# GpSimd's queue, in place of SP's, for the DRAM writes of the turned gates in a two-layer encoder trunk

## Chip, core and metric

The kernel runs on one NeuronCore of a Trainium2 chip. Its engines are TensorE (PE, with its weight loads shown apart as PEld), VectorE (DVE), ScalarE (ACT), GpSimd (POOL) and SyncE (SP); each takes its instructions in order and waits at semaphores. A DMA is issued by an instruction on some engine's queue, and instructions behind that one on the same engine follow it. The metric is the device time of one execution in microseconds, lower is better.

## What is computed

The reference runs a hidden state `h` of 256 tokens by 1024 channels through two layers, each a sandwich of feed-forward, mixer, feed-forward; the mixer is a convolution module in layer 0 and latent attention in layer 1. The change concerns the four feed-forwards:

```python
def swiglu_ffn(h, w1, w3, w2):
    return (jax.nn.silu(h @ w1) * (h @ w3)) @ w2
...
h = h + FFN_RES_WEIGHT * swiglu_ffn(rmsnorm(h, ffn_norm1[i]), ffn1_w1[i], ffn1_w3[i], ffn1_w2[i])
m = rmsnorm(h, mix_norm[i])
h = h + (conv_module(m, ...) if i % 2 == 0 else mla(m, positions, ...))
h = h + FFN_RES_WEIGHT * swiglu_ffn(rmsnorm(h, ffn_norm2[i]), ffn2_w1[i], ffn2_w3[i], ffn2_w2[i])
```

`w1` and `w3` are 1024 x 2816, `w2` is 2816 x 1024, all float32, and each is read from DRAM once.

## The kernel before

**Weights.** All weights stand in one list of blocks of 128 x 2048 float32 (1 MB) in the order of use. `load` (line 161) brings a block from DRAM into one of three `raw` buffers with a DMA on SP's queue (line 179), then splits it in two halves of 128 x 1024: ACT casts `hi` (line 187) and DVE takes the rest, `lo = raw - hi` (line 188), into one of five pairs of buffers. Each product is three TensorE instructions (`mm3`, lines 271 to 277): hi by low, hi by high, lo by high.

**A feed-forward** (`ffn_in`, line 637) has two stages. In the first, six chunks of gate columns are computed: `u = h @ w1` and `h @ w3` for two blocks of 128 tokens (tb 0 and 1), 512 columns in each of chunks 0 to 4 (four PSUM banks each), and 256 columns of both in chunk 5 (two banks). When a chunk's products are done, ACT takes silu from PSUM (`s`, line 721), DVE multiplies by the second half from PSUM (line 722), and `turn` (line 639) brings the gate into the layout with gate columns on the partitions. In the second stage `Rows` (line 570) multiplies the turned gates `Gh`, `Gl` by `w2` into four PSUM banks `o`, one for each token block and half of the output columns. The products `u`, `o` share the four banks of tag "A": the banks of `o(tb 1, d)` are those that chunk 5's two `u` tiles have just left.

**Turning a gate.** `turn_blocks` (line 344) turns a gate of 128 tokens by 512 columns in three steps. DVE transposes its 32 x 32 blocks (line 349) into `gt` (two buffers). Four DMAs (lines 352 and 353), one for each 32 partitions and of 64 KB, or 32 KB in chunk 5, write these blocks to a DRAM tile `gd` in rearranged order, as 32 x 4 pieces of 512 bytes. One DMA (line 357) reads the DRAM tile back as `gb`; it waits until the four writes have landed. Back in `turn`, ACT casts `Gh` from `gb` (line 646) and DVE subtracts for `Gl` (line 647). There are 12 gates in a feed-forward, thus 48 writes and 12 reads, and four feed-forwards: 192 writes and 48 reads. The same function, with the tag "h", turns part of `h` in front of three later stages (lines 404 to 411).

**The order.** A scheduler lays out each engine's instructions ahead of time, with some orders given by hand (`order`, `urgent`). So SP's queue is a fixed list of weight loads, gate writes and gate reads, and it stands still at the first one whose wait isn't met. DVE and ACT have fixed lists too, in which `Gh` and `Gl` stand between the casts of weights and the gates of the following chunk. GpSimd has little to do in the feed-forwards: a few 128 x 1 steps of norms, and in the first feed-forward 32 products `dpair` (line 1402) for the convolution.

Of the kernel before, what the change touches and what calls it, by code (L numbers as in the profile page):

```python
# [84 lines left out]
def trunk(ctx: ExitStack, tc: tile.TileContext, x, xt, first, pos, invf, gfin, wdw,  # L85
          f1w13, f1w2, f2w13, f2w2, cw1, cw2, wa, wuq, wukv, wo, wpair, out):
    nc = tc.nc
# [12 lines left out]
    def uid(s):  # L100
        n_uid[0] += 1
        return f"{s}_{n_uid[0]}"
# [34 lines left out]
    def order(ins, first):  # L137
        tc.add_manual_dep(ins.ins, first.name, mybir.DependencyInfo(
            mybir.DependencyClass.NoSync, mybir.DependencyReason.DATA), reason="order")
# [102 lines left out]
    for k in range(KT):  # L242
        c = slice(k % 4 * 512, k % 4 * 512 + 512)
# [100 lines left out]
    def turn_blocks(pool, src, n, tag, after=()):  # L344


        w = n * P
        t = pool.tile([P, 512], F32, tag=tag + "t", name=uid(tag + "t"), bufs=2)
        nc.vector.transpose(t[:, :w], src.rearrange("p (t j q) -> p j t q", t=n, q=32))  # L349
        d = dram.tile([P, w], F32, tag=tag + "d", name=uid(tag + "d"), bufs=4)  # L350
        dv = d.rearrange("(j p) (i c) -> i p j c", p=32, c=32 * n)
        for i in range(4):
            dma = nc.sync.dma_start(dv[i], t[32 * i:32 * i + 32, :w].rearrange("p (j c) -> p j c", j=4))
            for a in after:
                order(dma, a.ins)
        b = pool.tile([P, 512], F32, tag=tag + "b", name=uid(tag + "b"), bufs=2)
        last_read[0] = nc.sync.dma_start(b[:, :w], d)
        return b[:, :w].rearrange("p (i t q) -> p t i q", i=4, q=32)

    class Norm:  # L360
# [42 lines left out]
        @urgent  # L403
        def begin(self):

            raw_to(len(loaded) + RAW_BUFS)
            first = [dma for raw, dma in raws.values()]
            for q in range(2):
                self.turning.append(turn_blocks(self.pool, h[1][:, 512 * q:512 * q + 512], 4, "h", first))
                first = [last_read[0]]  # L410
                turns.extend(first)
# [225 lines left out]
    def ffn_in(act, X, make_next, beside):  # L637
        Gh = act.tile([P, NF, S], F32R, tag="Gh", name=uid("Gh"))
        Gl = act.tile([P, NF, S], F32R, tag="Gl", name=uid("Gl"))
        def turn(c, tb, w, g):  # L640

            n = w // P
            f = slice(4 * c, 4 * c + n)
            bv = turn_blocks(act, g[:, :w], n, "g")
            gh = Gh[:, f, tbs(tb)].rearrange("p t (i q) -> p t i q", q=32)
            nc.scalar.copy(gh, bv)  # L646
            nc.vector.tensor_sub(Gl[:, f, tbs(tb)].rearrange("p t (i q) -> p t i q", q=32), bv, gh.bitcast(F32))  # L647
# [874 lines left out]
```

## Time and profile before

| | |
|---|---|
| time, median of 3 runs | 918.64 us (918.57 to 919.02) |
| the profiled execution's own time | 918.66 us |
| its span, first to last instruction | 916.9 us |
| TensorE, weight loads, VectorE, ScalarE, GpSimd busy | 99%, 83%, 64%, 54%, 14% |
| DRAM traffic | 179.78 MB read, 14.16 MB written, 212 GB/s over the span |
| DMA queues | q1 "hardware_dynamic" moves 193.28 of 194.73 MB |

The profile shows one execution. A row of a timeline gives start, duration, engine, line, operation, the tile written and the tiles read, and how many such instructions were merged; the bracket behind it is the engine's idle time before it, with what ended it. "SPq" is a DMA issued on SP's queue, and its duration is that of the issue alone: the landing stands in a list of issues by line. A group's row gives the count, the total busy time, the mean of one in ns, and the idle time before. The "chain" of the profile goes back from the last instruction to what released each one.

### The profile page before, as it was taken

How to read it: one execution, taken by the hardware profiler on the slowest of the kernel's cores; microseconds unless marked ns; L12 is line 12 of the kernel's file. 1: busy time of each engine (PE TensorE's matmuls, PEld its weight loads, DVE VectorE, ACT ScalarE, POOL GpSimd, SP SyncE). 2: the span in 40 equal slices, each digit the busy share in tenths (PEclk: the TensorE clock that was granted, in tenths of full speed). 3: DMA queues.
4: the chain of work that ended last, by engine and by line, in shares of the span. 5: the costliest groups of instructions: out<-in, count | busy, mean ns of one | idle time of the engine just before them, and what ended most of it. 6: DMA issues, size and time to landing. Idle time of an engine off the chain costs nothing.

```text
span 916.9 us, 12087 instructions
## 1 busy us (share of the span) xinstructions
PE 908.8 (99%) x4337; PEld 764.4 (83%) x4337; DVE 590.8 (64%) x932; ACT 494.2 (54%) x845; POOL 126.8 (14%) x259
## 2 busy tenths in 40 slices
PE   9999999999999999999999999999999999999997
PEld 7888888898988888888888888888899888888886
DVE  6886764489987666655476666544768676566633
ACT  7564544388877444543364544434677574454432
POOL 1730000079951000000010000000400000000000
PEclk9999999999999999999999999999999999999999
DMA  9988776533227767776567777753445477776711
GB/s 332 315 271 284 265 265 218 193 138 139 93 77 269 251 230 236 251 232 221 184 212 267 246 247 241 234 209 135 156 155 184 147 253 277 249 250 219 255 48 46
DMA packets 65292, 194.73 MB, mean 212 GB/s; under 512 B 11728, under 2 KB 37200, under 8 KB 45904
## 3 DMA queue, kind: packets, MB, share of 16 engines
q1 hardware_dynamic: 64800, 193.28, 60.6%
q10 hardware_dynamic: 432, 0.69, 0.2%
q8 instruction: 34, 0.56, 0.2%
q14 instruction: 26, 0.21, 0.1%
HBM read 179.78 MB, written 14.16 MB: 212 GB/s over the span
## 4 chain that ended last, share of the span: by engine, by line
PE 97%; DMA 1%; ACT 0%; SPq 0%; DVE 0%; issue 0%; ACTq 0%
PE u L277 17%; PE u L273 17%; PE u L276 17%; PE o L277 10%; PE o L276 10%; PE o L273 10%; PE u L760 3%; PE gate L760 3%; PE o L995 2%; PE tp L317 1%; PE pairs L803 1%; DMA raw<-in_f1w 1%; PE a L276 1%; PE a L273 1%; PE a L277 1%; PE nope L277 1%
## 5 line engine op out<-in xcount | busy, mean ns | idle before, releaser
L188 DVE TENSOR_TENSOR lo<-raw,hi 128x1024 fp32r<-128x1024 f32 (+1 forms) x292 | 344.4, 1219 | 172.5 <-ACT hi L187 171.7
L187 ACT CAST hi<-raw 128x1024 fp32r<-128x1024 f32 x294 | 292.6, 1047 | 240.6 <-PE o L277 82.0
L273 PE MATMUL u<-lo,Xh 128*128 128x512 f32 x688 | 268.0, 389 | 0.2 <-DVE lo L188 0.2
L276 PE MATMUL u<-hi,Xh 128*128 128x512 f32 x688 | 267.7, 389 | 0.0
L277 PE MATMUL u<-hi,Xl 128*128 128x512 f32 x688 | 267.6, 389 | 0.0
L273 PEld LDWEIGHTS u<-lo,Xh 128*128 128x128 f32 x688 | 129.1, 188 | 27.3 <-DVE lo L188 0.6
L277 PEld LDWEIGHTS u<-hi,Xl 128*128 128x128 f32 x688 | 129.1, 188 | 27.2 <-DVE Xl L336 0.5
L276 PEld LDWEIGHTS u<-hi,Xh 128*128 128x128 f32 x688 | 129.1, 188 | 26.8
L276 PE MATMUL o<-hi,Gh 128*128 128x512 f32 (+1 forms) x356 | 137.9, 387 | 0.0
L277 PE MATMUL o<-hi,Gl 128*128 128x512 f32 (+1 forms) x356 | 137.8, 387 | 0.0
L273 PE MATMUL o<-lo,Gh 128*128 128x512 f32 (+1 forms) x356 | 137.2, 387 | 0.0
L308 POOL TENSOR_TENSOR ms<-ss 128x1 f32<-128x1 f32 x16 | 9.2, 576 | 586.6 <-ACT junk L300 586.6
L276 PEld LDWEIGHTS o<-hi,Gh 128*128 128x128 f32 x356 | 66.9, 188 | 13.6
L273 PEld LDWEIGHTS o<-lo,Gh 128*128 128x128 f32 x356 | 66.9, 188 | 13.5
L277 PEld LDWEIGHTS o<-hi,Gl 128*128 128x128 f32 x356 | 66.9, 188 | 13.4
L647 DVE TENSOR_TENSOR Gl<-gb,Gh 128x512 fp32r<-128x512 f32 (+1 forms) x48 | 31.3, 652 | 61.0 <-ACT Gh L646 61.0
L646 ACT CAST Gh<-gb 128x512 fp32r<-128x512 f32 (+1 forms) x48 | 28.0, 583 | 78.4 <-DMA gb<-gd 78.4
L849 DVE SCALAR_TENSOR_TENSOR acc<-V,dw,acc 128x128 f32<-128x128 f32 (+1 forms) x174 | 53.9, 390 | 0.0
L870 ACT ACTIVATE prod<-V,dw 128x128 f32<-128x128 f32 (+1 forms) x128 | 45.6, 416 | 1.8 <-POOL Y L871 1.0
L722 DVE TENSOR_TENSOR s<-s,u 128x512 f32<-128x512 f32 (+1 forms) x48 | 30.5, 634 | 7.6 <-PE u L277 7.6
L721 ACT ACTIVATE s<-u,R 128x512 f32<-128x512 f32 (+1 forms) x48 | 31.2, 649 | 5.0 <-PE u L277 3.7
L349 DVE STREAM_TRANSPOSE gt<-s 128x512 f32<-128x512 f32 (+1 forms) x48 | 32.0, 666 | 1.4
(222 smaller groups left out, 858.6 us busy)
## 6 DMA issues: line engine op xcount, KB each, us to landing
raw<-in_f2w SPq DMA_DIRECT2D x66, 1024.0 KB, 5.0
raw<-in_f1w SPq DMA_DIRECT2D x62, 1024.0 KB, 5.3
raw<-in_cw SPq DMA_DIRECT2D x12, 1024.0 KB, 4.8
gd<-gt SPq DMA_DIRECT2D x160, 64.0 KB, 3.5
gb<-gd SPq DMA_DIRECT2D x40, 256.0 KB, 4.6
raw<-in_wo SPq DMA_DIRECT2D x4, 1024.0 KB, 4.9
raw<-in_wuq SPq DMA_DIRECT2D x3, 1024.0 KB, 4.7
raw<-in_f1w SPq DMA_DIRECT2D x8, 256.0 KB, 4.7
```

The source lines that it names most:

```text
L187: casts[len(loaded), i] = (nc.scalar.copy(hi[:, c], raw[:, c]), low.tensor_sub(lo[:, c], raw[:, c], hi[:, c].bitcast(F32)))
L188: low.tensor_sub(lo[:, c], raw[:, c], hi[:, c].bitcast(F32)))
L273: mm = nc.tensor.matmul(o, ah, bl, start=start, stop=False)
L276: nc.tensor.matmul(o, ah, bh, start=False, stop=False)
L277: return nc.tensor.matmul(o, al, bh, start=False, stop=stop)
L349: nc.vector.transpose(t[:, :w], src.rearrange("p (t j q) -> p j t q", t=n, q=32))
L647: nc.vector.tensor_sub(Gl[:, f, tbs(tb)].rearrange("p t (i q) -> p t i q", q=32), bv, gh.bitcast(F32))
L721: nc.scalar.activation(s[:, :w], u[0, tb][:, :w], AF.Silu, scale=X.r[tb])
L722: nc.vector.tensor_mul(s[:, :w], s[:, :w], u[0, tb][:, w:] if both else u[1, tb])
L760: mm = nc.tensor.matmul(u[:, t], w[:, c], X.x[:, k, t], start=(k == 0), stop=(k == KT - 1))
L849: dve_last.append(nc.vector.scalar_tensor_tensor(out if j == j1 - 1 else y, v, w, y, op0=ALU.mult, op1=ALU.add))
L870: prods_last.append(nc.scalar.activation(p, v, AF.Copy, scale=w))
```

## The change

One line of `turn_blocks` chooses the queue of the four writes: GpSimd's for gates (tag "g"), SP's for `h`. The read (line 357, now 359) and all weight loads stay in SP's queue.

```diff
@@ -350,7 +350,9 @@
         d = dram.tile([P, w], F32, tag=tag + "d", name=uid(tag + "d"), bufs=4)
         dv = d.rearrange("(j p) (i c) -> i p j c", p=32, c=32 * n)
         for i in range(4):
-            dma = nc.sync.dma_start(dv[i], t[32 * i:32 * i + 32, :w].rearrange("p (j c) -> p j c", j=4))
+
+            queue = nc.gpsimd if tag == "g" else nc.sync
+            dma = queue.dma_start(dv[i], t[32 * i:32 * i + 32, :w].rearrange("p (j c) -> p j c", j=4))
             for a in after:
                 order(dma, a.ins)
         b = pool.tile([P, 512], F32, tag=tag + "b", name=uid(tag + "b"), bufs=2)
```

The scheduler lays out the lists anew. TensorE's list is the same but for three products of `o(0, 0)` in each feed-forward, which now stand behind the first products of `o(1, 0)`. On SP, the 192 writes are gone, and each pair of gate reads stands about one weight load later than before. On ACT and DVE the steps `Gh`, `Gl` of a gate stand later by one cast of a weight block or one gate step. On GpSimd the writes stand in order of the gates; in the first feed-forward 12 of the 32 `dpair` products stand between chunk 0's two gates and 20 between its second gate and chunk 1's writes.

## Prediction

> **What bounds the kernel now.** I read the page first (busy shares, clock, chain), then TensorE's waits, then the waits of ACT and of SP's queue.
>
> ```profile
> span 916.9 us, 12087 instructions
> ...
> PE 908.8 (99%) x4337; PEld 764.4 (83%) x4337; DVE 590.8 (64%) x932; ACT 494.2 (54%) x845; POOL 126.8 (14%) x259
> ...
> PEclk9999999999999999999999999999999999999999
> ...
> PE 97%; DMA 1%; ACT 0%; SPq 0%; DVE 0%; issue 0%; ACTq 0%
> ```
> ```profile
> PE warm L265 <- DVE still L260: 1.0, 1, 1.0
> PE u L282 <- ACT Xh L457: 0.8, 1, 0.8
> PE u L273 <- DVE lo L188: 0.2, 1, 0.2
> ```
>
> TensorE is busy from the first products to the last at the full granted clock, it is 97% of the chain that ends last, and all its waits come to 2.0 us, at the start. So nothing that SP, POOL, ACT or DVE do less of can shorten the span by more than about 2 us, while each of them can lengthen it once its work reaches TensorE too late. The question is how much slack stands between a gate and its use.
>
> ```profile
> ACT Gh L646 <- DMA gb<-gd: 78.4, 33, 7.6
> ...
> ACT hi L187 <- PE u L277: 67.3, 25, 3.4
> ```
> ```profile
> SPq L179 <- DVE lo L188: 398.1, 95, 15.7
> ...
> SPq L357 <- DMA gd<-gt: 25.6, 42, 2.8
> ```
>
> The casts of weights (hi, L187) wait for TensorE to leave a buffer, and the loads (SP, L179) wait 398.1 us for a raw buffer: weights run ahead as far as the buffers allow. The other rows are the loop of the gates: SP waits for writes to land, and ACT waits 33 times for a read.
>
> **The change part by part.** *Removed:* 192 writes leave SP's queue. There a write takes half a microsecond (eight in 3.96 us, next fence: 0.495 us each), some 95 us of SP in all. As SP only waits to load ahead and TensorE does not wait for weights, this is worth nothing; at most it is the 2.0 us above.
>
> *Added:* 192 writes on POOL, idle in the feed-forwards but for the dpair products of the first. What is late next is seen by following one gate. The following rows are from the second feed-forward, at the end of its first stage: SP, ACT, DVE, then TensorE.
>
> ```profile
> 344.43 3.97 SPq L353 DMA_DIRECT2D gd<-gt  x8
> ...
> 366.19 4.14 SPq L353 DMA_DIRECT2D gd<-gt  x8
> ...
> 387.95 3.96 SPq L353 DMA_DIRECT2D gd<-gt  x8
> 392.57 0.34 SPq L357 DMA_DIRECT2D gb<-gd  x1
> ```
> ```profile
> 393.97 2.01 ACT L187 CAST hi<-raw 128x1024 fp32r<-128x1024 f32 x2 [3.39 <-PE u L277]
> 395.87 0.62 ACT L646 CAST Gh<-gb 128x512 fp32r<-128x512 f32 x1
> ```
> ```profile
> 386.49 0.68 DVE L722 TENSOR_TENSOR s<-s,u 128x512 f32<-128x512 f32 x1
> 387.21 0.71 DVE L349 STREAM_TRANSPOSE gt<-s 128x512 f32<-128x512 f32 x1
> ...
> 395.05 2.36 DVE L188 TENSOR_TENSOR lo<-raw,hi 128x1024 fp32r<-128x1024 f32 x2 [2.85 <-ACT hi L187]
> 397.33 0.69 DVE L647 TENSOR_TENSOR Gl<-gb,Gh 128x512 fp32r<-128x512 f32 x1
> ...
> 400.19 0.41 DVE L722 TENSOR_TENSOR s<-s,u 128x256 f32<-128x256 f32 x1
> ```
> ```profile
> 404.65 0.39 PE L273 MATMUL o<-lo,Gh 128*128 128x512 f32 x1
> ```
>
> A full chunk takes 387.95 - 366.19 = 21.76 us (and 21.76 from 344.43). DVE's list in the changed program runs, per chunk: Gl of the first gate, two lo, Gl of the second gate, two lo, then the next chunk's gate. So a late second read holds up the next gate on DVE, and that gate's writes are later again: the wait is fed back. Write T for the time that one write takes on POOL, W for the time from its issue's end to its landing, r for a read's issue to landing. From the end of one chunk's first transposition to that of the next the loop takes: eight writes on POOL, 8T (the second gate's transposition, 2 us later, is ready before POOL comes to it); W; the read's issue, 0.34; r; Gh 0.62; ACT's two hi 2.01 with the second lo 1.2 behind; the gate 0.68; the transposition 0.71. Together 8T + W + r + 5.5.
>
> ```profile
> gd<-gt SPq DMA_DIRECT2D x160, 64.0 KB, 3.5
> gb<-gd SPq DMA_DIRECT2D x40, 256.0 KB, 4.6
> ```
>
> From these medians W = 3.5 - 0.5 = 3.0 and r = 4.6 (the read stands behind a 1 MB weight load in SP's queue). No trace here shows T: POOL issues no DMA before. One end is SP's own 0.5 us. For the other I take POOL's rows by size.
>
> ```profile
> L871 POOL TENSOR_TENSOR Y<-Y,prod 128x256 f32<-128x256 f32 x15 | 10.8, 721 | 0.0
> ...
> L188 POOL TENSOR_TENSOR lo<-raw,hi 128x1024 fp32r<-128x1024 f32 x2 | 4.7, 2356 | 1.8 <-ACT hi L187 1.8
> ```
>
> POOL's longest comparable piece takes 2.36 us: the other end. A write has 32 x 4 = 128 pieces of 512 bytes; if POOL itself has to name the source and the target of each piece, an address and a length, that is 512 words. Between 256 elements in 0.72 us and 1024 in 2.36, 512 take 1.27 us. I take T = 1.27: an estimate from rows of another operation, between 0.5 and 2.36.
>
> The loop then takes 10.2 + 3.0 + 4.6 + 5.5 = 23.3 us, 1.5 over TensorE's 21.76, and over the four hand-overs between the five full chunks the gate falls 6.0 us behind. Behind chunk 5 stands o(1, 1), which needs the bank that chunk 5's last gate leaves (DVE 400.19, L722). In the changed program this gate stands behind Gh and Gl of chunk 4's first gate alone, that is 4T + W + 0.34 + r + 0.62 + 0.69 + 0.41 and 0.1 of gaps = 14.8 us after the transposition's end (387.92). TensorE first writes that bank at 404.65, 16.7 us after it. So 6.0 + 14.8 - 16.7 = 4.1 us of stall a feed-forward, 12 us for the last three.
>
> The first feed-forward starts worse, since POOL also has the dpair products.
>
> ```profile
> 29.60 1.82 SPq L353 DMA_DIRECT2D gd<-gt  x4
> ...
> 55.62 1.76 SPq L353 DMA_DIRECT2D gd<-gt  x4
> ...
> 115.06 4.18 SPq L353 DMA_DIRECT2D gd<-gt  x8
> ```
> ```profile
> 30.40 22.78 POOL L1402 TENSOR_TENSOR dpair<-dpair,wpair 128x192 f32<-128x192 f32 x32 [6.27 <-DMA wpair<-in_wpair]
> ```
>
> In POOL's new list stand 4 writes, 12 dpair, 4 writes, 20 dpair, then chunk 1's writes: 29.6 + 5.1 + 8.5 + 5.1 + 14.2 = 62.5, 6.9 us after chunk 1's gate (55.6). The first hand-over has no casts between Gl and the transposition: 10.2 + 3.0 + 0.34 + 4.6 + 0.62 + 0.69 + 0.71 = 20.2. Two more at 23.3 bring chunk 4's gate to 55.6 + 6.9 + 20.2 + 46.6 = 129.3 against 115.06: 14.2 behind, less the 1.9 of slack at the end (16.7 - 14.8): 12 us.
>
> The sum is 12 + 12 = 24 us. The profiled execution took 918.66 us, 1.8 more than its span, and stands at the median (918.64): 918.7 + 24 = 943. The three moved products of o(0, 0) cost nothing (the same products on the same banks), nor do SP's waits for eight more semaphores at the end, met long before.
>
> Weights are covered: SP standing longer at the reads delays loads by a few microseconds, while the casts still wait 67.3 us for TensorE's buffers. This cover goes with the loop, not before it.
>
> **A rule of the skill against the row.** SP's row shows 0.495 us an issue and 3.5 to land. The Trainium skill's page "DMA: Bandwidth & Descriptors", section "Anatomy of one DMA — SWDGE (gpsimd) path", gives a DMA from GpSimd about 2.0 us of fixed time, most of it waiting for the write's receipt and not set-up. By that rule the price lies in W and T is small, no run here shows it, and the time would be that of the first rival below.
>
> **The rivals.** *Hidden* (not slower). POOL issues about as fast as SP. With T = 0.5 the loop takes 4.0 + 3.0 + 4.6 + 5.5 = 17.1 us, under 21.76, and the first feed-forward's writes start 29.6 + 2 + 8.5 + 2 + 14.2 = 56.3, almost on time: 918.7. It decides where T falls under the point at which the first feed-forward's stall is gone: at T = 0.9 chunk 1's writes start at 59.5, chunk 4's gate comes at 55.6 + 3.9 + 17.2 + 2 x 20.3 = 117.3, 2.2 behind, less 3.4 of slack: nothing; at T = 1.0 it is about 2 us. For it: POOL has no other work in three feed-forwards, and the times W and r are medians of rows in which SP's own queue was full. Against it: each small POOL step costs 0.2 to 0.6 us already.
>
> *DVE holds POOL up.* Where both work, DVE's rows grow:
>
> ```profile
> 27.73 1.22 DVE L188 TENSOR_TENSOR lo<-raw,hi 128x1024 fp32r<-128x1024 f32 x1
> ...
> 48.70 1.33 DVE L188 TENSOR_TENSOR lo<-raw,hi 128x1024 fp32r<-128x1024 f32 x1
> ```
>
> The second ran beside dpair. If each write had to let one such DVE instruction pass, T = 1.27 + 1.2 = 2.5: the loop takes 33.1, 45 us are lost in four hand-overs and 3 at the end, 48 a feed-forward: some 1110 us. The small growth (0.1 us) speaks against it. The skill's page "SBUF — State Buffer", section "SBUF: two separate sides", says that GpSimd can't write its DMA descriptors while DVE runs a two-port operation, a copy for instance; L188 isn't one, so by the page this does not happen here.
>
> *Faster.* SP's queue is free of 95 us of issues and loads start earlier, which could only take part of the 2.0 us of waits, or some of the tail: 917.
>
> **How the numbers follow.** Slower by the loop, T between about 1 and 1.7: 0.55. Hidden: 0.37. DVE holds POOL up: 0.05. Faster: 0.03. With T = 1.7 the loop takes 26.7: 19.7 us a feed-forward in the last three, about 30 in the first, 1008 us. The range goes from 917.8 (hidden) to 1005; above it lie the rest of the first case and the DVE rival, some 0.12. About 0.2% is what a measurement of this kernel can tell from no change: faster by over that 0.03, within 0.37, slower 0.60.
>
> **What would show it.** POOL's row of the writes gives T, the list of issues W. If the loop binds, TensorE's waits show u or o released by DVE s (L724), at the first products of o(1, 0) and o(1, 1) of each feed-forward, most in the first; ACT's wait of Gh for gb grows far over 78.4 us. If hidden, TensorE's busy time stays 908.8 and its waits 2.0. It would be wrong in mechanism if TensorE came to wait for lo or hi, or if the clock row fell.

## The result, and the profile after

| | before | after |
|---|---|---|
| median of 12 runs | 918.61 us (918.13 to 919.71) | 920.66 us (920.12 to 921.36) |
| ratio, 95% interval | | 1.0021, 1.0014 to 1.0029 |
| profiled execution: its time, its span | 918.66, 916.9 us | 920.65, 918.8 us |

The changed kernel is 2.05 us slower, 0.2%. The stalls that were forecast (24 us) are not there. The page of the changed kernel:

```profile
span 918.8 us, 12243 instructions
...
PE 909.3 (99%) x4337; PEld 764.8 (83%) x4337; DVE 591.7 (64%) x932; ACT 497.6 (54%) x845; POOL 231.2 (25%) x451
...
PEclk9999999999999999999999999999999999999998
...
PE 97%; DMA 1%; ACT 0%; SPq 0%; DVE 0%; issue 0%; ACTq 0%
```

TensorE's waits in the changed kernel:

```profile
PE warm L265 <- DVE still L260: 1.1, 1, 1.1
PE u L273 <- DVE lo L188: 0.3, 1, 0.3
```

TensorE is as busy as before (909.3 against 908.8 us) and waits less (1.4 against 2.0). Now the group of the writes on GpSimd (count, busy us, mean ns of one, idle before them), then the list of issues with landings, then GpSimd's timeline in the second feed-forward:

```profile
L355 POOL DMA_DIRECT2D gd<-gt x192 | 104.5, 552 | 333.0 <-DVE gt L349 316.7 <-PE u L277 13.7 <-issue 2.6
```
```profile
gd<-gt POOLq DMA_DIRECT2D x160, 64.0 KB, 3.2
gb<-gd SPq DMA_DIRECT2D x40, 256.0 KB, 5.2
```
```profile
344.58 4.33 POOL L355 DMA_DIRECT2D gd<-gt  x8 [17.42 <-DVE gt L349]
366.34 4.33 POOL L355 DMA_DIRECT2D gd<-gt  x8 [17.43 <-DVE gt L349]
388.10 4.33 POOL L355 DMA_DIRECT2D gd<-gt  x8 [17.44 <-DVE gt L349]
```

A write takes GpSimd 0.54 us (4.33 / 8), the chunks follow each other at 21.76 us as before, and GpSimd stands idle for 17.4 us in each. So the loop does not bind, and the loss is elsewhere. TensorE's last product ends at 910.72 us after and at 910.79 before: everything up to there is equal, and the 1.9 us by which the spans differ stand behind it. There the timeline shows only the closing norm and the outputs' DMAs, at the same times in both to 0.07 us. What differs is seen when the rows of the program's last line are asked for by line: instructions of the engines' sequencers, with count, shortest / median / longest in ns, and start of the first and last. Before, then after:

```profile
L1510 POOLq DRAIN  x3: 34/78/397, 910.7 to 916.6; - x3
L1510 SPq DRAIN  x3: 7/7/7, 916.1 to 916.4; - x3
```
```profile
L1512 POOLq DRAIN  x3: 34/102/7445, 910.6 to 918.6; - x3
L1512 SPq DRAIN  x3: 7/7/7, 916.0 to 918.3; - x3
```

At the end of a program each engine drains and then all meet. SP is there at 916.0 to 916.1 in both kernels, when the outputs have landed. GpSimd's first drain starts at 910.6, while its last instruction (an addition of the closing norm, 910.68 to 910.96) still runs. Before it took 0.40 us and GpSimd was early. After it takes 7.45 us, to 918.08, and everybody waits for it: 918.08 - 916.04 (SP's last drain in front of the meeting) = 2.0 us, the whole loss.

### The profile page after: what moved, and what is told of

The parts are those of the page before. It is cut to its first block, busy times and chain, and to the rows that moved or that the text cites. A ratio compares the mean times of both kernels' runs of the same rounds, so it can differ in the third digit from the quotient of the medians.

```text
span 918.8 us, 12243 instructions
## 1 busy us (share of the span) xinstructions
PE 909.3 (99%) x4337; PEld 764.8 (83%) x4337; DVE 591.7 (64%) x932; ACT 497.6 (54%) x845; POOL 231.2 (25%) x451
## 2 busy tenths in 40 slices
DMA packets 43790, 194.74 MB, mean 212 GB/s; under 512 B 7633, under 2 KB 12625, under 8 KB 24401
## 4 chain that ended last, share of the span: by engine, by line
PE 97%; DMA 1%; ACT 0%; SPq 0%; DVE 0%; issue 0%; ACTq 0%
PE u L273 17%; PE u L277 17%; PE u L276 17%; PE o L277 10%; PE o L276 9%; PE o L273 9%; PE u L762 3%; PE gate L762 3%; PE o L997 2%; DMA raw<-in_f1w 1%; PE tp L317 1%; PE pairs L805 1%; PE a L273 1%; PE a L277 1%; PE a L276 1%; PE nope L277 1%
## 5 line engine op out<-in xcount | busy, mean ns | idle before, releaser
L355 POOL DMA_DIRECT2D gd<-gt x192 | 104.5, 552 | 333.0 <-DVE gt L349 316.7
L723 ACT ACTIVATE s<-u,R 128x512 f32<-128x512 f32 (+1 forms) x48 | 31.2, 651 | 17.1 <-PE u L277 16.3
```

Source lines behind the costliest of these rows:

```text
L355: dma = queue.dma_start(dv[i], t[32 * i:32 * i + 32, :w].rearrange("p (j c) -> p j c", j=4))
L723: nc.scalar.activation(s[:, :w], u[0, tb][:, :w], AF.Silu, scale=X.r[tb])
```

## The experiments

Two questions: what sets the length of that drain, and how far the forecast loop was from binding. Where a table gives a "remainder", it is the end of GpSimd's first closing drain (start plus duration) less the end of GpSimd's last instruction, from the trace: 0.07 us before, 7.12 after.

**One write on GpSimd.** The first of the 192 writes goes there, the rest stay on SP (`one` is a list that holds GpSimd's queue once).

```diff
-            queue = nc.gpsimd if tag == "g" else nc.sync
+            queue = one.pop() if one and tag == "g" else nc.sync
```

> Only the first of the 192 gate writes goes to GpSimd's queue; the other 191 stay on SP's. The trace of the changed kernel shows GpSimd's closing drain at 7.445 us, from 910.63 to 918.08, where it took 0.397 us before, and everything else of the tail done at 916.06. Theory A, a closing price that is paid once as soon as GpSimd has issued any DMA: the drain takes 7.4 us here too, the time is 920.7 (+2.0). Rival B, a price per write (drain time or queue time that grows with the number of writes): 7.05 us / 192 is 0.04 us for one write, the drain stays near 0.4 us and the time is 918.6. Rival C, the drain waits for something left by the last write (recency): the last GpSimd write is 880 us before the end, the drain stays near 0.4 us, 918.6.

Measured: 918.52 us, ratio 0.9997 (0.9988 to 1.0006). The drain's row:

```profile
L1513 POOLq DRAIN  x3: 34/89/493, 910.2 to 916.3; - x3
```

0.49 us: no price for the mere use of the queue. Theory A falls.

**GpSimd done earlier.** The last two GpSimd instructions of the program go to VectorE.

```diff
-                nc.gpsimd.tensor_scalar(e, q, EPS if self.e[tb] is None else self.e[tb], None, op0=ALU.add)
+                (nc.gpsimd if tb == 0 else nc.vector).tensor_scalar(e, q, EPS if self.e[tb] is None else self.e[tb], None, op0=ALU.add)
```

> The changed kernel, with the two last 128x1 additions of the closing norm (fe of the second token block) on VectorE in place of GpSimd. GpSimd's last instruction is then the power R at 907.09 + 0.57 = 907.66, 3.0 us earlier, so its drain starts near 907.2 to 907.7. Theory A (a fixed 7.4 us from the start of the drain, whatever is left to do): the drain ends at 914.6 to 915.2, ahead of the last output's landing (SP's waits end at 916.06 before, 915.9 after), and the time falls to that of before, 918.6. Rival D, GpSimd's drain ends at a fixed distance behind the end of the other work (it waits for the last output or for the DMA engines to be idle): the drain grows to 10.5 us, 920.7 stays. Rival B/C make no difference between the two: 920.7.

Measured: 918.55 us, ratio 0.9997 (0.9988 to 1.0006).

```profile
L1512 POOLq DRAIN  x3: 34/102/7723, 907.4 to 916.9; - x3
L1512 SPq DRAIN  x3: 7/7/7, 916.3 to 916.6; - x3
```

The drain is as long (its remainder behind GpSimd's last instruction is 7.12 us again), but it starts 3.2 us earlier and ends at 915.2, ahead of SP's 916.3. The loss is gone. So the drain is a span of its own behind GpSimd's last instruction and does not wait for the other work. The control, the same move in the kernel before:

> The control of the run above: the same move of two additions to VectorE in the kernel before. GpSimd's drain took 0.4 us there and everybody waited for SP's outputs, so by theory A nothing changes: 918.6, within 0.3 us. If the move itself gains (GpSimd's 1.0 us steps off the closing norm's path), it shows here as well, and the gain in the run above has to be read less that.

Measured: 918.52 us, ratio 0.9999 (0.9990 to 1.0008). The move gains nothing by itself, and with the drain hidden all 192 writes on GpSimd are worth nothing either (918.55 against 918.54).

**Half of the writes.**

```diff
-            queue = nc.gpsimd if tag == "g" else nc.sync
+            queue = nc.gpsimd if tag == "g" and gates[0] <= 24 else nc.sync
```

`gates[0]` counts the gates; the second run has `> 24`.

> Only the first two feed-forwards' gates (96 writes) go to GpSimd's queue, the last two keep SP's. GpSimd's closing drain took 0.397 us with no write on its queue, 0.493 with one (the first of the kernel) and 7.445 with 192. Theory B (a price collected in the drain that grows with the number of DMAs, 7.05 / 192 = 0.037 us each): 0.4 + 96 x 0.037 = 3.9 us, which ends at 914.5, ahead of the last output's 916: time 918.6. Rival C (only what the last feed-forward left counts): 0.4 to 0.5 us, 918.6. Rival A (a fixed price from some small number of DMAs on): 7.4 us, 920.7. The time alone does not tell B from C; the drain does.

> Only the last two feed-forwards' gates (96 writes) go to GpSimd's queue. Theory B: the drain takes 3.9 us as in the run with the first two, and ends at 914.5: 918.6. Rival C (recency): 7.4 us, 920.7. Rival A: 7.4 us in both, 920.7.

Measured: 921.15 us (1.0027, 1.0016 to 1.0037) and 921.29 us (1.0029, 1.0018 to 1.0039): dearer than all 192. The rows of the first and of the last half:

```profile
L1514 POOLq DRAIN  x3: 34/102/8265, 910.5 to 919.3; - x3
```
```profile
L1514 POOLq DRAIN  x3: 34/93/8263, 910.6 to 919.4; - x3
```

The two agree to 2 ns, so recency (C) falls; 96 cost more than 192, so B in its plain form falls too, and A had fallen already.

**Each write cut in two.**

```diff
-            dma = queue.dma_start(dv[i], t[32 * i:32 * i + 32, :w].rearrange("p (j c) -> p j c", j=4))
+            tv = t[32 * i:32 * i + 32, :w].rearrange("p (j c) -> p j c", j=4)
+            k = 2 if tag == "g" else 1
+            for j in range(0, 4, 4 // k):
+                dma = queue.dma_start(dv[i][:, j:j + 4 // k], tv[:, j:j + 4 // k])
```

> The changed kernel with each gate write cut in two (two of the four column blocks each): 384 DMAs on GpSimd with the same bytes and the same 24576 pieces of up to 512 bytes. Theory B by DMA: the drain takes 0.4 + 384 x 0.037 = 14.5 us, ends near 925.1 and the time is 927.7 (+7 over the changed kernel), if no stall comes with it. Theory B by piece or byte: the drain stays 7.4 us, 920.7. For the loop: if a DMA costs GpSimd 0.54 us whatever its pieces, a chunk's writes take 16 x 0.54 = 8.7 us, as with T = 1.08 of the prediction, and the loop of 8.7 + 2.7 + r + 5.5 stays at or under 21.76 for r up to 4.9: no stall in the last three feed-forwards, 0 to 5 us in the first. If it goes by pieces, each takes 0.27 and nothing changes.

Measured: 918.88 us, ratio 0.9999 (0.9989 to 1.0008), with 384 DMAs of 0.536 us each: GpSimd's time for a DMA goes by the DMA and not by its pieces. 16 of them fill 8.6 us of a chunk, and TensorE waited for nothing but its first product. And the drain:

```profile
L1515 POOLq DRAIN  x3: 34/102/2137, 910.5 to 917.0; - x3
```

Neither 14.5 nor 7.4 us: both forms of B missed. A price that rises, falls and rises again suggested a store that fills by DMAs and is emptied on the way (theory S). Four kernels followed, each run once, with the queue chosen by a counter of writes (`queue = nc.gpsimd if tag == "g" and left[0] > 0 else nc.sync`).

> The first 48 gate writes (the first feed-forward) on GpSimd's queue, the rest on SP's. The closing drain lasted 0.40 us with no write on GpSimd's queue, 0.49 with one, 8.26 with 96 (the first or the last 96 alike), 7.45 with 192, and 2.14 with 384 of half the pieces: so neither fixed, nor growing with the number, nor a matter of recency. Theory S (sawtooth): the price counts how far a store of fixed size has been filled since it last began anew, (8.26 - 0.49) / 95 = 0.082 us a write; 192 writes then stand 86 writes into a second round, which puts the round at 106 writes. For 48 writes: 0.49 + 47 x 0.082 = 4.3 us of drain, 918.6. Rival L (some level of 7 to 8 us that sets in early, with an irregular part): 7 to 8 us, 920.7 to 921.3.

> The first 110 gate writes on GpSimd's queue. Theory S with a round of 106 writes: 4 writes into the second, a drain of 0.7 us and 918.6, the same price as hardly any write. Rival L, or a price that falls slowly from 8.26 at 96 to 7.45 at 192: 8.1 us, 921.2.

> The first 144 gate writes on GpSimd's queue. Theory S: 38 into the second round, 0.41 + 38 x 0.082 = 3.5 us, 918.6. Rival L or slow fall: 7.9 us, 921.

> The first 48 gate writes on GpSimd's queue, each cut in two: 96 DMAs of half the pieces. Theory S says that the price goes by what a DMA puts into the store. By DMA: 8.26 us as with 96 whole writes, 921.2. By pieces: 4.3 as with 48 whole ones, 918.6. By pieces and one entry for the end of each DMA on each of 16 engines (8 + 1 against 4 + 1): 96 x 5/9 x 0.082 + 0.4 = 4.8 us, 918.6.

Measured, in this order: 918.21, 922.75, 919.03 and 921.36 us (before: 918.45). 110 writes missed S by far, with the longest drain of all:

```profile
L1514 POOLq DRAIN  x3: 34/102/9407, 910.8 to 920.7; - x3
```

48, 144 and the 96 halves came as S said, the last by the count of DMAs. Two kernels run ten times each, then three run once, were to find where it begins anew.

> The first 127 gate writes on GpSimd's queue, the other 65 on SP's. GpSimd's part of the closing beyond its last instruction was 0.07 us with no DMA on its queue, 0.17 with 1, 4.10 with 48, 7.94 with 96 (whole or half ones), 9.08 with 110, then 3.20 with 144, 7.12 with 192 and 1.81 with 384: 0.082 us a DMA, and after 128 it begins anew from 1.8. Theory S with a round of 128 DMAs: 0.08 + 127 x 0.082 = 10.5 us here, GpSimd ends at 911.0 + 10.5 = 921.5 where SP ends at 916.0, so the time is 918.5 + 5.5 = 924.0. Rival: the round ends somewhere between 111 and 126 DMAs, by the size of what is stored and not by their count: 1.8 to 3 us, 918.5.

> The first 128 gate writes on GpSimd's queue, one more than in the run beside it. Theory S with a round of 128: GpSimd's closing takes 1.8 us beyond its last instruction and ends at 912.8, under SP's 916.0: 918.5, some 5.5 us less than with 127. If the round ends only with the 129th: 10.5 us, 924.1.

Measured: 918.40 us (0.9999, 0.9990 to 1.0008) and 918.52 us (1.0002, 0.9993 to 1.0012). The step of 5.5 us between 127 and 128 is not there: both stand behind the break.

> The first 126 gate writes on GpSimd's queue. Beyond GpSimd's last instruction the closing took 1.81 us with 127 and 1.89 with 128, 3.20 with 144 and 7.12 with 192, which is 1.81 + 0.082 x (n - 127). If a round is 127 DMAs by count, 126 still stands in the first: 0.08 + 126 x 0.082 = 10.4 us, GpSimd ends at 921.4 and the time is 923.9, the dearest of all. If the round had ended earlier: 1.73 us, 918.5.

> The first 120 gate writes on GpSimd's queue. A round of 121 or more: 0.08 + 120 x 0.082 = 9.9 us, GpSimd ends at 920.9 and the time is 923.4. A round that ends between 111 and 120: 1.81 - 7 x 0.082 = 1.2 us, 918.5.

> The first 96 gate writes on GpSimd's queue, each cut in two: 192 DMAs of half the pieces. 96 such halves were priced as 96 whole writes (7.93 us beyond GpSimd's last instruction). A round by count: as 192 whole ones, 7.1 us, 920.7. A round by what is stored, with twice the room for halves: 0.08 + 192 x 0.082 = 15.8 us, GpSimd ends at 926.8 and the time is 929.3.

Measured: 919.06, 919.23 and 919.29 us (before: 918.36); their drains end at 912.9, 912.5 and 916.7. Only the third ends behind SP's (915.9). The first two were run once, and the drain does not explain their excess of 0.7 to 0.9 us; the 12 runs of the kernel before range as far (918.13 to 919.71). The third fits neither of its two forecasts: its remainder is 5.89, where 7.1 or 15.8 was expected. All remainders, in us:

| DMAs on GpSimd's queue | remainder | 0.08 + 0.0818 x | with x = |
|---|---|---|---|
| 0 | 0.07 | | |
| 1 | 0.17 | 0.16 | 1 |
| 48 | 4.10 | 4.01 | 48 |
| 96 (first half, last half, 48 cut in two) | 7.94, 7.94, 7.93 | 7.93 | 96 |
| 110 | 9.08 | 9.08 | 110 |
| 120 | 1.24 | 1.23 | 14 = 120 - 106 |
| 126, 127, 128 | 1.73, 1.81, 1.89 | 1.72, 1.80, 1.88 | 20, 21, 22 |
| 144 | 3.20 | 3.19 | 38 = 144 - 106 |
| 192 | 7.12 | 7.11 | 86 = 192 - 106 |
| 192 halves (96 cut in two) | 5.89 | 5.89 | 71 = 192 - 121 |
| 384 halves | 1.81 | 1.80 | 21 = 384 - 3 x 121 |

Each DMA adds 0.082 us to the closing, whether it is a whole write or half of one. Between the 111th and the 120th whole write, 106 of them leave the bill at once; with half writes 121, once by 192 and three times by 384. The trace shows where. GpSimd has one long pause among the 192 writes of the changed kernel, in front of the 114th (the first of these eight is the 113th), and it waits there for nothing that the profile shows ("issue"):

```profile
525.05 0.55 POOL L355 DMA_DIRECT2D gd<-gt  x1 [17.42 <-DVE gt L349]
528.07 3.80 POOL L355 DMA_DIRECT2D gd<-gt  x7 [2.48 <-issue]
```

All seven kernels here with more than 113 whole writes and nothing put between them pause for 2.47 to 2.48 us in front of the 114th; those with 110 and fewer have no such pause. With 384 halves it stands in front of the 250th and of the 371st, 121 apart:

```profile
553.96 2.11 POOL L358 DMA_DIRECT2D gd<-gt  x4 [2.47 <-issue]
853.59 2.64 POOL L358 DMA_DIRECT2D gd<-gt  x5 [2.75 <-issue]
```

And in both kernels with halves the 129th, another 121 ahead, starts 3.23 us behind its transposition, where 0.29 is usual when GpSimd stands idle. 113 - 106 and 128 - 121 both leave 7. So theory S holds in its outline: at 113 whole or 128 half writes GpSimd stops for some 2.5 us, and all but 7 leave the bill, for which the closing would have taken 106 x 0.082 = 8.7 us (an estimate). TensorE does not wait for it. That the pause does the taking off is read from these counts and was not tested by itself; why the number is 113 with whole writes and 128 with halves stays open.

**How far the loop was from binding.** 0.57 us of GpSimd work (a 128 x 1 power into a spare column) is put behind each write after the order is laid out, so that everything else stands as in the changed kernel; once, and twice in the second run (`range(2 * ...)`, `range(2)`). `pad` is the spare tensor, `writes` the places of the gate writes in the laid out list.

```diff
+        for i in range(1 * len(writes)):
+            col = pad[:, i % 128:i % 128 + 1]
+            nc.gpsimd.tensor_tensor(col, pad[:, 128:], pad[:, 128:], op=ALU.pow)
...
+        for i in reversed(writes):
+            planned[i + 1:i + 1] = [work.pop() for _ in range(1)]
```

> The changed kernel with one more GpSimd instruction behind each gate write, a 128x1 power into a spare column (0.57 us by the rows of R<-ms,neghalf); the order of all other instructions on every engine is that of the changed kernel. It makes a write cost T = 0.54 + 0.57 + about 0.08 = 1.19 us of GpSimd, near the 1.27 that the prediction had taken. By the prediction's sum with the measured W = 2.65 and r = 5.2: loop 9.5 + 13.4 = 22.9 against 21.76, 4.6 us behind after four hand-overs, less 1.9 of slack, 2.7 us for each of three feed-forwards, and 11 in the first (chunk 1's writes 6.8 late): +19, 940 us, with TensorE waiting for s of VectorE at the first products of o(1, 0) and o(1, 1). Rival: the loop has more play than the sum allows (r or the casts shorten when nothing queues): no stall, 920.7.

Measured: 927.44 us, ratio 1.0094 (1.0079 to 1.0109): 6.8 over the changed kernel, neither 19 nor nothing. Part of the miss is T: from start to start a write took 1.13 us here (median) and not 1.19, and with 1.13 the expectation's sum gives 9 us in place of 19, 8 of them in the first feed-forward. TensorE's waits, and its clock around the only stall (stretch, its length, busy us of PE, PEld, DVE, ACT, POOL, then the granted clock, the DMA share and GB/s):

```profile
PE o L273 <- DVE s L724: 4.3, 1, 4.3
```
```profile
130.00:135.00 5.00, 1.53 (x7) 0.94 (x5) 0.70 (x2) 0.90 (x3) 4.04 (x9) 1.00 0.68 208
135.00:139.00 4.00, 3.18 (x8) 2.55 (x9) 3.97 (x6) 2.76 (x5) 3.97 (x6) 0.57 0.59 226
139.00:150.00 11.00, 11.00 (x50) 9.13 (x49) 6.11 (x8) 6.12 (x8) 3.66 (x6) 1.00 0.65 216
```

The stall is where the prediction looked for it (o(1, 1), by VectorE's s), in the first feed-forward alone. 4.3 us are waiting; the next products run at 0.57 of the clock, and TensorE's busy time grows from 909.3 to 911.3. In the other three the loop held. A term that the sum took as fixed gave way:

```profile
gb<-gd SPq DMA_DIRECT2D x40, 256.0 KB, 2.8
```

The read lands in 2.8 us in place of 5.2, and with 2.8 the loop is 20.0 us, under 21.76. The rows on SP fit a read that comes late enough to find the weight loads done: one at 382.31 us is issued 5.1 us behind the last load's issue, one in the changed kernel (392.62) 0.2 us behind it. This was not tested by itself.

> The changed kernel with two powers behind each gate write, all other orders as in the changed kernel. One power made T = 1.19 us (eight writes in 9.5) and a first feed-forward with one stall of 4.4 us, none in the other three: 927.44, where the sum had said 940. In that run the read took r = 2.8 in place of 5.2 (median), as it came late enough to find SP's queue empty. With two, T = 1.19 + 0.57 + 0.03 = 1.79 and a chunk's writes take 14.3. By the sum with r = 2.8: loop 14.3 + 2.8 + 2.8 + 5.5 = 25.4, 3.6 a chunk, 14.6 behind after four; the end's chain 4 x 1.79 + 2.8 + 0.34 + 2.8 + 1.8 = 14.9 against 16.7 of slack: 12.8 us in each of the last three feed-forwards, about 20 in the first: 920.7 + 58 = 979. With r = 5.2 kept it is 24 and 33: 1026. Rival, the loop does not bind at all and only the first feed-forward stalls: 935.

Measured: 975.83 us, ratio 1.0621 (1.0594 to 1.0647). TensorE's waits:

```profile
PE o L273 <- DVE s L724: 25.7, 8, 3.7
PE u L273 <- ACT s L723: 3.1, 3, 1.6
PE u L273 <- DVE s L724: 3.0, 2, 2.3
```
```profile
PE 930.1 (96%) x4337; PEld 774.9 (80%) x4337; DVE 593.0 (61%) x932; ACT 491.3 (51%) x845; POOL 501.2 (52%) x836
...
PEclk9999989999999999979999999899999999999898
```

Now all four feed-forwards stall, at the first products of o(1, 0) and o(1, 1), and the first at products of u as well (5.6 us). The total is near the 979 that was expected, but made differently: 6.5 to 7.0 us of waits in each of the last three, where 12.8 were expected, and 31.5 in all beyond the changed kernel's. A write took 1.68 us from start to start (median), not the 1.79 aimed at; with 1.68 and the read's 2.7 us of this run the sum gives 7.6 us, near what was measured, and with the read's 5.2 kept it gives 20. The other 20.8 us of the span's 52.3 are TensorE running slower behind the stalls (busy 930.1 against 909.3).

## Why the prediction was wrong

- *What bounds the kernel; SP's relief is worth nothing.* Right. With GpSimd's drain out of the way the kernel takes 918.55 against 918.54 us, though SP no longer issues 192 writes. Its wait for a raw buffer only grew, from 398.1 to 484.0 us:

```profile
SPq L179 <- DVE lo L188: 484.0, 109, 15.7
```

- *"I take T = 1.27: an estimate from rows of another operation."* This is the step that failed. Measured: 0.54 us from write to write, next to the end that SP's own row gave. The argument behind it, 512 words for 128 pieces, is refuted by the halves: 64 pieces cost the same 0.54. Between two ends far apart the nearest row was that of a DMA issue on another engine, and not that of elementwise work. With T = 0.54 the prediction's own sum gives 8 x 0.54 + 2.7 + 5.2 + 5.5 = 17.7 us, as the first rival did (17.1), against 21.76: no stall (W = 3.2 - 0.5 and r from the list of issues). The Trainium skill's page "DMA: Bandwidth & Descriptors", section "Anatomy of one DMA — SWDGE (gpsimd) path", which puts the price into the receipt and not into the set-up, agrees with this trace as far as the set-up goes: 0.54 us of GpSimd, 3.2 to land. That the rest is the receipt no run here shows.
- *The loop.* The mechanism and its place were right: with T raised to 1.13 and 1.68 the stalls stand at the products named, released by VectorE's s. Its size comes out near once T and r are those of the run: 7.6 us a feed-forward by the sum, 6.5 to 7.0 of waits measured. r is no fixed term, though: it fell from 5.2 to 2.8 as the gates came later. T = 1.27 itself was not run; a straight line between the two runs (6.8 and 55.2 us over the changed kernel) gives 19 us for it, an estimate, where the forecast had 24. Left out altogether was that TensorE runs slower behind a stall.
- *The first feed-forward's dpair.* Right that it starts worse: with T = 0.54, chunk 1's writes start at 57.34 us, where the Hidden rival had worked out 56.3, and the single stall at T = 1.13 is in this feed-forward.
- *"nor do SP's waits for eight more semaphores at the end, met long before".* True as it stands: SP is there at 916.0 as before. But only SP's closing was considered. GpSimd's, 0.40 us in the trace of before, became 7.45, and 2.0 us of it stand out. No step of the prediction contained this term. It takes the place of all others in the result, and the *Hidden* rival's 918.7 misses it too.
- *DVE holds POOL up.* Not seen: writes of 0.55 us, none but the first (0.78) over 0.63, beside a VectorE that is busy 64% of the span.
- *The range* (917.8 to 1005) holds 920.66, as its lower end reached to *Hidden*. That the kernel is slower at all, as was forecast, is luck: the 2.0 us come from the closing drain and not from the loop.

## What to carry to other kernels

Where the cost of an operation on one engine isn't in the trace, look first at the row of the same operation on another engine: here it was the nearer neighbour (0.495 us against 0.54), and another operation on the same engine was far off (1.27). When a queue is put to use for the first time, look at the end of the program too: ask which engine is last at the closing drain, and how much room lies between its last instruction and the last output's landing. A feedback loop's terms, taken from a run in which everything queues, can shrink when the loop runs late, so that a sum over them comes out too high, while the clock's loss behind each stall is not in it at all.

## What the runs showed of the hardware that was not expected

- GpSimd's closing drain grows by 0.082 us with each DMA on its queue (0.49 us with 1, 8.26 with 96, 9.41 with 110), by their count and not by their bytes, and falls when 106 whole or 121 half writes leave at once: 1.56 us with 120, 7.45 with 192. It costs time only where it ends behind the last output.
- In front of the 114th whole write GpSimd pauses for 2.48 us, and with halves 2.5 to 2.8 in front of the 250th and the 371st; the closing drain no longer counts the writes that leave there.
- A DMA issued by GpSimd takes it 0.54 us with 128 pieces or with 64.
- GpSimd's writes move in longer packets: the page counts 43790 packets after against 65292 before, 12625 against 37200 of them under 2 KB, at the same 194.7 MB. With the drain out of the way the time is that of before (918.55 against 918.54).
- Behind a stall of 4.3 us TensorE's granted clock was 0.57 over the stretch from 135 to 139 us. With two powers, the four stalls of 0.5 to 1.6 us left it at 1.00 over the 4 us behind them, and the nine of 2.3 to 3.7 us were followed by 0.50 to 0.68.
